# Hybrid attention block on one core: in the last unit the tensor engine keeps the program's order, with new places for transposes and products

## The chip, the cores and the metric

The kernel runs on one core of one Trainium2 chip. The metric is device time in microseconds of one execution, as the median of the runs shown. The core has four computing engines that matter here. TensorE does matrix products and transposes (PE in the profile, its weight loads PEld). VectorE (DVE) and ScalarE (ACT) move and compute elementwise. GpSimd (POOL) and SyncE (SP) mostly start DMAs. Each engine works off its own instructions in the order in which they stand in the program and waits at an instruction until what that instruction needs is there.

## The reference

The input is 512 tokens of width 1024, with 16 meta tokens put ahead. After a layer norm, one projection gives all that two attention branches and their gates need. The part that the change touches is the stick-breaking branch and what uses its result:

```python
def stick_breaking_block(q, k, v, q_pos):
    before = k_pos[None, :] < q_pos[:, None]
    z = jnp.einsum('bhqd,bhkd->bhqk', q, k) * (SB_HEAD_DIM ** -0.5)
    log_keep = jnp.where(before, jax.nn.log_sigmoid(-z), 0.0)
    suffix = lax.cumsum(log_keep, axis=3, reverse=True) - log_keep
    a = jnp.where(before, jnp.exp(jax.nn.log_sigmoid(z) + suffix), 0.0)
    return jnp.einsum('bhqk,bhkd->bhqd', a, v)
...
br_d = (y_d * silu(g_d)) @ w_br_diff
br_s = (y_s * silu(g_s)) @ w_br_sb
merged = sigmoid(m_d + b_gate[0]) * br_d + sigmoid(m_s + b_gate[1]) * br_s
h = layer_norm(DN_ALPHA * h + merged @ w_out, ln_g, ln_b)[:, N_META:]
```

## The kernel before

**Numbers and products.** Every float32 operand of a large product is split into a rounded part and a rest: a weight block `raw` gives `wh` (ScalarE, L183) and `wl` (VectorE, L188). A product is then three matmuls, high by high, high by rest and rest by high. One block is half of a projection, and `prep` splits it four blocks ahead of its use. A projection of 128 columns (`proj_tok`, L494 to L496) is 24 matmuls of 128x512 into one PSUM bank `ps`. Its pool `pj` has three banks.

**Units.** The attention is sixteen units: eight heads of the first branch (`d`), then eight pairs of heads of the stick-breaking branch (`s`). While a unit's attention runs, TensorE also computes projections for later units, and `run(proj, steps)` mixes the two. Each `yield` of a projection advances a clock of the program's own, and each step has a number on that clock at which it is written into the program. The numbers are in units of that clock and are no device times.

**One pair of heads.** For each of the two heads `c` of an `s` unit, `s_scores` makes logits in bank `sc` (L754), two sigmoids on ScalarE (L901, L903), a scan on VectorE (L907) and the attention weights `apad` (L908). `transposed` returns three parts: part 0 transposes four blocks into `t0` (L766), part 1 strips and three blocks into `t1` (L784, L766), part 2 three blocks into `t2`. After each part, ScalarE copies the bank to `ah` and VectorE subtracts to `al` (L771, L772), and part 2 also leaves a float32 block `af` (L802). The banks come from the pool `ptp`, which has two. `s_values` multiplies by the values into the single bank `av` (L916 to L924), ScalarE copies one half of it (`half`, L928), and VectorE adds (L930).

**The last unit.** It has no next unit to project for. Its five projections are `gd` 7, `md` 0, 1 and 2, and `gs` 7 (a gate projection, whose `silu` is L523, L524 and L526). Head `c`'s parts 0, 1, 2 stand at 7.0, 7.7 and 8.4 plus 6.5 times `c`, its product at 10.5 plus 6.5 times `c`.

**The late stage.** Behind the units, the attention's memory is given back (`early.close()` and the end of the pool `att`), and the pool `late` takes its place. First come seven projections, `md` 3 to 7 and `ms` 0 and 1, into `td` and `sm` by a sigmoid (L565). Mixed with them, `operands` builds from the finished first branch `ydT` four parts of `gh` and `gl` for the products of L1062: four elementwise steps on VectorE (L1037 to L1040), three casts to `gh` on ScalarE (L1043), and three subtractions to `gl` on VectorE (L1044).

**What sets the order.** Tile sorts the instructions of each engine by dependencies and expected times, so an instruction of the program may slip behind later ones. `follow` ties an instruction behind another of its engine. `keep_order(first, engines)` (L233) does so for all instructions from place `first` on: each keeps its place in the program's order on its engine. It is called for the start of the kernel and, for all engines, for the late stage. The units between are left to the sorting. The tie of the late stage binds its own instructions to each other, not to what is left of the last unit.

## Time and profile before

| | |
|---|---|
| median of 3 runs | 714.28 us (713.76 to 714.56) |
| the profiled execution | 716.97 us, of which 714.6 us are the span from first to last instruction |
| mean granted TensorE clock | 0.993 of full speed |
| TensorE busy | 698.9 us |
| VectorE busy | 571.8 us |
| ScalarE busy | 439.1 us |
| traffic | 123.36 MB by DMA |

In the views, start times count from the start of the span. A timeline row gives start, duration, engine, line, operation, output and inputs, and in brackets the idle time of the engine just before it and what ended it. A matmul's duration covers its way through the array, and the next one starts while it is still under way, so the pace of matmuls is read from start to start. In the views by window, PEclk is the granted share of TensorE's clock.

### The profile page before, as it was taken

Reading aid. Unit: us, or ns where it says so; the run is one execution under the profiler, and the core shown is the slowest. Engines: PE = TensorE matmul, PEld = TensorE weight load, DVE = VectorE, ACT = ScalarE, POOL = GpSimd, SP = SyncE. Lnnn points to the kernel's source line nnn. Section 1 sums busy time; section 2 is a strip of 40 time slices with the busy share of each in tenths; the row PEclk is TensorE's granted clock in tenths of the full one; section 3 lists DMA queues with packets and bytes.
Section 4 is the critical chain, followed back from the end, with each engine's and each line's share of the span. In section 5 each row is a group of like instructions: output and inputs, shape, how many; then the busy total and the mean of one; then the engine's idle time right before and its main releaser. Section 6 shows DMA issues by size and latency. Waiting matters only on the chain.

```text
span 714.6 us, 13390 instructions
## 1 busy us (share of the span) xinstructions
PE 698.9 (98%) x4494; PEld 637.0 (89%) x4494; DVE 571.8 (80%) x1265; ACT 439.1 (61%) x1065; POOL 125.9 (18%) x143
## 2 busy tenths in 40 slices
PE   8999999999999999999999999999989999999994
PEld 7999999989989898998989898888878998999884
DVE  6888898878788678988968989876296788788887
ACT  5776676757667687776848768666265446555300
POOL 3204210212222101212213110000012102130002
PEclk9999999999999999999999999999999999999998
DMA  9358854879987976999799875748249748696902
GB/s 292 95 166 164 177 129 121 185 180 192 191 204 167 225 178 154 192 208 217 197 205 197 203 171 139 199 113 253 79 130 181 150 126 185 136 191 174 321 15 103
DMA packets 182182, 123.36 MB, mean 173 GB/s; under 512 B 9009, under 2 KB 165074, under 8 KB 182114
## 3 DMA queue, kind: packets, MB, share of 16 engines
q1 hardware_dynamic: 148130, 102.32, 50.0%
q0 software_dynamic: 33664, 19.14, 21.4%
q10 hardware_dynamic: 320, 1.06, 0.4%
q8 instruction: 35, 0.57, 0.4%
q14 instruction: 33, 0.27, 0.1%
HBM read 91.96 MB, written 9.44 MB: 142 GB/s over the span
## 4 chain that ended last, share of the span: by engine, by line
PE 83%; DVE 8%; DMA 4%; ACT 3%; issue 1%; POOL 1%; SPq 0%; DVEq 0%; ACTq 0%; POOLq 0%
PE q L690 15%; PE ps L494 11%; PE ps L495 11%; PE ps L496 11%; PE q L1062 10%; PE ps L510 7%; PE sc L754 5%; PE t L766 3%; PE bank L385 1%; PE tv L723 1%; DMA raw<-in_w_in_dram 1%; DMA raw<-in_w_out_dram 1%; DMA lgb<-in_ln_g_dram 1%; DVE hr L1212 1%; DMA xt<-in_x_dram 1%
## 5 line engine op out<-in xcount | busy, mean ns | idle before, releaser
L494 PE MATMUL ps<-hTh,wh 128*128 128x512 f32 x368 | 145.5, 395 | 1.8 <-ACT wh L183 1.8
L188 DVE TENSOR_TENSOR wl<-raw,wh 128x512 fp32r<-128x512 f32 x169 | 115.5, 691 | 38.0 <-ACT wh L183 36.0
L495 PE MATMUL ps<-hTl,wh 128*128 128x512 f32 x368 | 145.3, 395 | 0.0
L496 PE MATMUL ps<-hTh,wl 128*128 128x512 f32 x368 | 145.2, 394 | 0.0
L183 ACT CAST wh<-raw 128x512 fp32r<-128x512 f32 x169 | 104.4, 625 | 30.2 <-PE ps L495 17.3
L494 PEld LDWEIGHTS ps<-hTh,wh 128*128 128x128 f32 x368 | 69.5, 189 | 15.4 <-ACT wh L183 2.2
L496 PEld LDWEIGHTS ps<-hTh,wl 128*128 128x128 f32 x368 | 69.6, 189 | 14.3 <-DVE wl L188 0.4
L495 PEld LDWEIGHTS ps<-hTl,wh 128*128 128x128 f32 x368 | 69.5, 189 | 13.4
L146 POOL DMA_DIRECT2D rawk<-in_w_in_dram x44 | 61.1, 1649 | 95.2 <-DMA rawk<-in_w_in_dram 50.5
L754 PE MATMUL sc<-k,A 128*128 128x264 f32 (+3 forms) x320 | 66.4, 300 | 0.0
L1062 PE MATMUL q<-gh,wh 128*128 128x256 f32 x224 | 63.5, 283 | 0.2 <-ACT t L1071 0.2
L1062 PE MATMUL q<-gl,wh 128*128 128x256 f32 x224 | 63.4, 283 | 0.0
L1062 PE MATMUL q<-gh,wl 128*128 128x256 f32 x224 | 63.4, 283 | 0.0
L907 DVE TENSOR_TENSOR_SCAN e<-e,diag 128x528 f32<-128x528 f32 (+1 forms) x64 | 53.5, 848 | 7.3 <-ACT e L901 7.2
L754 PEld LDWEIGHTS sc<-k,A 128*128 128x128 f32 x320 | 50.5, 189 | 3.2
L690 PE MATMUL q<-tS,wh 128*128 128x264 f32 x176 | 50.9, 290 | 0.9 <-DVE low L612 0.9
L690 PE MATMUL q<-tl,wh 128*128 128x264 f32 x176 | 50.2, 286 | 0.0
L690 PE MATMUL q<-tS,wl 128*128 128x264 f32 x176 | 50.2, 286 | 0.0
L772 DVE TENSOR_TENSOR al<-t,ah 128x512 fp32r<-128x512 f32 (+2 forms) x72 | 39.7, 552 | 12.5 <-ACT ah L771 8.6
L771 ACT CAST ah<-t 128x512 fp32r<-128x512 f32 (+2 forms) x72 | 34.2, 477 | 21.3 <-PE t L766 21.1
L510 PE MATMUL ps<-hTh,wh 128*128 128x264 f32 x160 | 46.4, 290 | 0.2 <-ACT k L632 0.2
L933 POOL DMA_DIRECT2D ys<-half x14 | 11.8, 840 | 196.2 <-ACT ys L932 109.7
(291 smaller groups left out, 1867.0 us busy)
## 6 DMA issues: line engine op xcount, KB each, us to landing
raw<-in_w_in_dram SPq DMA_DIRECT2D x141, 256.0 KB, 3.3
rawk<-in_w_in_dram POOLq DMA_DIRECT2D x44, 256.0 KB, 5.7
rawk<-in_w_in_dram SPq DMA_DIRECT2D x33, 256.0 KB, 3.8
k<-ks SPq DMA_DIRECT2D x60, 132.0 KB, 2.9
raw<-in_w_out_dram SPq DMA_DIRECT2D x16, 256.0 KB, 3.7
k<-ks SPq DMA_DIRECT2D x60, 66.0 KB, 2.6
A<-low SPq DMA_DIRECT2D x28, 128.0 KB, 3.0
raw<-in_w_br_diff_dram SPq DMA_DIRECT2D x12, 256.0 KB, 4.0
```

The lines of the kernel that those rows point to most:

```text
L146: second[l] = [lambda raw=raw, x=x: g.dma_start(raw, x, accum_op=ALU.add) for x in more]
L183: s.copy(wh, raw)
L188: eng.tensor_tensor(wl, raw, wh.bitcast(F32), op=ALU.subtract)
L494: pe.matmul(ps, wh[:, k % 4, :], hTh[:, k, M:], start=(k == 0), stop=False)
L495: pe.matmul(ps, wh[:, k % 4, :], hTl[:, k, M:], start=False, stop=False)
L496: pe.matmul(ps, wl[:, k % 4, :], hTh[:, k, M:], start=False, stop=(k == KT - 1))
L510: pe.matmul(ps[:, :H2], a[:, k % 4, :], b[:, k, ts(c, H2)], start=(k == 0 and m == 0), stop=(k == KT - 1 and m == 2))
L690: pe.matmul(bank, a[:, k, :], b, start=start and k == 0 and j == 0, stop=k == 3 and j == 2, skip_group_check=not start)
L754: pe.matmul(ps[:, :n], q, K[:, m, k0:k0 + n], start=(m == 0), stop=(m == 1))
L772: v.tensor_tensor(l, t[:, o:o + w], h.bitcast(F32), op=ALU.subtract)
L907: v.tensor_tensor_scan(rev, rev, diag[0][:, L - nk:][:, ::-1], 0.0, ALU.mult, ALU.max)
L1062: pe.matmul(bank, a[:, k, :], b[:, n, k, :], start=start and k == 0 and m == 0, stop=k == 3 and m == 2, skip_group_check=not start)
```

## The change

Two things are changed, both for the last unit alone. The steps of its two heads get numbers from a table `LAST` (parts 0, 1, 2 and the product, for each head): 13.0, 14.1, 18.2, 21.2 and 21.9, 21.9, 23.2, 24.9. And all instructions of TensorE (`ORDERED[:1]`) from the place in the program at 12.9 on keep the program's order, to the end of the kernel. The other engines are sorted in the last unit as they were.

```diff
+LAST = [13.0, 14.1, 18.2, 21.2], [21.9, 21.9, 23.2, 24.9]
...
                     parts = transposed(ta, apads[c])
-                    steps += [(7.0 + 6.5 * c + 0.7 * m, f) for m, f in enumerate(parts)]
-                    steps.append((10.5 + 6.5 * c, lambda c=c, ta=ta: s_values(unit, c, n, ta)))
+                    times = LAST[c] if last else [7.0 + 6.5 * c + 0.7 * m for m in range(3)] + [10.5 + 6.5 * c]
+                    steps += zip(times, parts)
+                    steps.append((times[3], lambda c=c, ta=ta: s_values(unit, c, n, ta)))
+                if last:
+                    steps.append((LAST[0][0] - 0.1, lambda: state.update(ends=len(nc.cur_bb.bb.instructions))))
             run(proj, steps)
...
+    keep_order(state["ends"], ORDERED[:1])
     keep_order(first, ORDERED + [mybir.EngineType.SP])
```

**The second head's product on TensorE.** In the kernel before, the product of head 1 (`av_6938`) is split: its first matmul L916 stands earlier, and the rest stands six matmuls into the third projection of the late stage (`ps_7121` is `md` 5, with `wh_7035` its first block):

```order
L494 MATMUL ps_7121<-hTh_149,wh_7035 128x512
L495 MATMUL ps_7121<-hTl_150,wh_7035 128x512
L496 MATMUL ps_7121<-hTh_149,wl_7036 128x512
L917 MATMUL av_6938<-af3_6919,v3_436 128x128
L918 MATMUL av_6938<-am_6898,v4_435 128x4x32
L922 MATMUL av_6938<-ah1_6900,V_6652 128x384
L923 MATMUL av_6938<-al1_6901,V_6652 128x384
L922 MATMUL av_6938<-ah2_6915,V_6652 128x256
L923 MATMUL av_6938<-al2_6916,V_6652 128x256
L924 MATMUL av_6938<-al0_6885,V_6652 128x512
```

In the changed kernel the same product (`av_6998`) stands in one piece, three matmuls ahead of the end of `gs` 7 (`ps_6916`), the last unit's last projection; six matmuls stand between the transposes of part 2 and it:

```order
L766 MATMUL t2_6982<-ident_129,apad1_434 128x128 x3
...
L496 MATMUL ps_6916<-hTh_149,wl_6818 128x512
L916 MATMUL av_6998<-ah0_6952,V_6652 128x512
L917 MATMUL av_6998<-af3_6990,v3_436 128x128
L918 MATMUL av_6998<-am_6963,v4_435 128x4x32
L922 MATMUL av_6998<-ah1_6965,V_6652 128x384
L923 MATMUL av_6998<-al1_6966,V_6652 128x384
L922 MATMUL av_6998<-ah2_6986,V_6652 128x256
L923 MATMUL av_6998<-al2_6987,V_6652 128x256
L924 MATMUL av_6998<-al0_6953,V_6652 128x512
```

Between the last place at which the two orders agree (the logits of 128x400 of head 1, L754) and the end of this product stand 120 projection matmuls before and 63 in the changed kernel. All else that stands there is the same work.

**ScalarE around it.** Before, the copy of head 1's product (`half_6947`) stands behind all else of the last unit and directly ahead of the late stage's first casts (`gh_7030`), which stand ahead of `md` 3's sigmoid (`td_7025`) and of the split of `md` 6's first block (`wh_7084`):

```order
L802 COPY af3_6919<-t2_6911 128x128
L928 COPY half_6947<-av_6938 64x512
L1043 CAST gh_7030<-ydT_6623 128x256
L1043 CAST gh_7030<-ydT_6623 128x2x256
L1043 CAST gh_7030<-t_7065 128x4x256
L565 ACTIVATE td_7025<-ps_7034,cols_144 128x512
L183 CAST wh_7084<-raw_6926 128x512
```

In the changed kernel the split of a block of `md` 5 (`wh_7053`) and the sigmoid of `gs` 7 (`sg_7013`) stand between the copy and the casts; from there on the order is as before. Ahead of the copy, the split `wh_7035` stands between the copies of part 1 and part 2:

```order
L771 CAST ah1_6965<-t1_6956 128x384
L183 CAST wh_7035<-raw_6801 128x512
L771 CAST ah2_6986<-t2_6982 128x256
L802 COPY af3_6990<-t2_6982 128x128
L928 COPY half_7007<-av_6998 64x512
L183 CAST wh_7053<-raw_6821 128x512
L523 ACTIVATE sg_7013<-ps_6916 128x512
L1046 CAST gh_7030<-ydT_6623 128x256
L1046 CAST gh_7030<-ydT_6623 128x2x256
L1046 CAST gh_7030<-t_7065 128x4x256
L565 ACTIVATE td_7025<-ps_7034,cols_144 128x512
L183 CAST wh_7084<-raw_6869 128x512
```

VectorE's rows follow the same pattern: the split `wl_7036` stands between part 1's `al` and part 2's `al`, and behind the sum L930 of head 1 stand `wl_7054`, the four elementwise steps and the two steps of the gate. GpSimd's and SyncE's rows stand in the same order in both kernels.

## Prediction

> **What bounds the kernel now.** I read the page first. It says which engine sets the time:

> ```profile
> span 714.6 us, 13390 instructions
> PE 698.9 (98%) x4494; PEld 637.0 (89%) x4494; DVE 571.8 (80%) x1265; ACT 439.1 (61%) x1065; POOL 125.9 (18%) x143
> ```

> TensorE is busy for 98% of the span, and the change takes no matmul away. So only stretches in which TensorE stands still, or runs below full clock, can be given back or added. The waits of TensorE alone, longest first, name the stretches:

> ```profile
> engine line waited for: us in total, times, longest us
> PE ps L494 <- ACT wh L183: 1.8, 1, 1.8
> PE warm L306 <- POOL ident masks.py:199: 1.4, 1, 1.4
> ```

> The longest wait of the whole kernel is one projection matmul that waits for a split weight block. The second row is the kernel's start. TensorE's timeline shows where the first one is:

> ```profile
> 516.83 0.39 PE L924 MATMUL av<-al,V 128*128 128x512 f32 x1
> 517.06 0.40 PE L494 MATMUL ps<-hTh,wh 128*128 128x512 f32 x1
> ...
> 520.96 0.39 PE L496 MATMUL ps<-hTh,wl 128*128 128x512 f32 x1
> 523.17 0.64 PE L494 MATMUL ps<-hTh,wh 128*128 128x512 f32 x1 [1.82 <-ACT wh L183]
> ...
> 526.66 0.46 PE L496 MATMUL ps<-hTh,wl 128*128 128x512 f32 x1
> 526.96 0.40 PE L494 MATMUL ps<-hTh,wh 128*128 128x512 f32 x1
> ```

> The first row is the end of the last unit's attention: the last matmul of head 1's product. Eighteen projection matmuls follow, then the wait, and behind it matmuls of 0.64 instead of 0.40 us. The windows around it say why:

> ```profile
> core 0: us, PE busy (x) PEld busy (x) DVE busy (x) ACT busy (x) POOL busy (x), PEclk, DMA share, GB/s
> 440.00:441.00 1.00, 0.64 (x5) 0.64 (x6) 1.00 (x3) 1.00 (x4) 0.00 (x0) 1.00 1.08 367
> 500.00:510.00 10.00, 10.00 (x51) 8.38 (x50) 3.59 (x7) 2.77 (x6) 0.00 (x0) 1.00 0.47 148
> 515.00:521.19 6.19, 6.19 (x31) 5.05 (x29) 3.16 (x7) 1.73 (x4) 0.00 (x0) 1.00 0.01 1
> 521.19:523.17 1.98, 0.16 (x1) 0.00 (x1) 1.80 (x3) 1.98 (x4) 0.00 (x0) 1.00 0.00 0
> 523.17:526.78 3.61, 3.61 (x9) 2.62 (x10) 3.26 (x8) 2.38 (x5) 0.00 (x0) 0.53 0.43 127
> ```

> The granted clock (PEclk) is 1.00 up to the wait and 0.53 for 3.6 us behind it. The wait costs twice: once standing still, once in a slow stretch. Why the block is late, ScalarE's and VectorE's timelines tell:

> ```profile
> 517.32 0.58 ACT L928 COPY half<-av 64x512 f32<-64x512 f32 x1 [5.75 <-PE av L924]
> 518.70 0.93 ACT L1043 CAST gh<-ydT 128x256 fp32r<-128x256 f32 x2 [0.81 <-DVE ysT L930]
> 520.98 1.04 ACT L1043 CAST gh<-t 128x1024 fp32r<-128x1024 f32 x1 [1.34 <-DVE t L1040]
> 521.93 0.68 ACT L565 ACTIVATE td<-ps,cols 128x512 f32<-128x512 f32 x1
> 522.51 1.12 ACT L183 CAST wh<-raw 128x512 fp32r<-128x512 f32 x2
> ...
> 517.93 0.69 DVE L930 TENSOR_TENSOR ysT<-av,half 64x512 f32<-64x512 f32 x1 [6.66 <-ACT half L928]
> 518.66 0.69 DVE L526 TENSOR_TENSOR ysT<-sg,ysT 128x512 f32<-128x512 f32 x1
> 519.27 0.42 DVE L1037 TENSOR_TENSOR t<-ydT 128x256 f32<-128x256 f32 x1
> ```

> ScalarE stands idle for 5.75 us until head 1's product is done, then copies it. The casts `gh` wait for VectorE's sum L930, which is the last reader of the memory that they go to, and only behind the casts and one sigmoid stand the splits `wh` for which TensorE waits. ScalarE had time for them, but they are queued behind a product that stands late on TensorE.

> **The change part by part.**

> *The wait.* First, what it costs. Without it, the matmul at 523.17 would have started one step after 520.96. A step is (520.96 - 517.06)/17 = 0.229 us. So 523.17 - 520.96 - 0.23 = 1.98 us are lost standing still. The nine slow matmuls take 526.96 - 523.17 = 3.79 us where nine steps take 2.06, and lose 1.73. Together 3.71 us.

> Then, whether it goes. From the last common place to the end of head 1's product, 63 projection matmuls stand instead of 120, and all else is equal. So the product ends 57 x 0.229 = 13.1 us earlier, with its last matmul's step at 517.06 - 13.1 = 504.0, if nothing new holds TensorE. The block `wh_7084` is the first of `md` 6, three projections or 72 matmuls behind `gs` 7. With three matmuls left of `gs` 7, it is needed at 504.0 + 75 x 0.229 = 521.2, as late as before, since the projections only trade places with attention work. When is it ready? The new rows ahead of it on ScalarE and VectorE take these durations, besides 0.69 for a split on VectorE (like L526):

> ```profile
> 501.92 0.59 ACT L523 ACTIVATE sg<-ps 128x512 f32<-128x512 f32 x1
> 502.65 0.69 DVE L524 TENSOR_TENSOR sg<-ps,sg 128x512 f32<-128x512 f32 x1
> ```

> The copy ends at 517.32 + 0.58 - 13.1 = 504.8. VectorE's queue from there is L930, the split `wl_7054`, two small steps, L524, one small step, L526 and one small step: 4 x 0.69 + 4 x 0.42 = 4.4 us, to 509.2. ScalarE's split and sigmoid lie within that. The last cast `gh` takes 1.04, to 510.3. Then the sigmoid `td` needs the end of `md` 3, at 504.0 + 27 x 0.229 = 510.2 and a matmul's way of 0.39: it ends about 511.3. The split ends half a microsecond later, at 511.9. That is 9 us ahead of 521.2. Before, it came 2 us too late. So the wait goes whole, with the slow stretch behind it: 3.7 us.

> What is late next? The other `gh` parts are queued on ScalarE behind sigmoids that follow TensorE's projections; each takes about 3 us with its waits, inside a projection's 24 x 0.229 = 5.5. The later blocks are split before the next part and stay ahead by about as much. Behind that, loads follow the freed buffers and so move with TensorE. I cost these at nothing; their cover is those 9 us.

> *The new order in the last unit.* TensorE now takes each transpose and each product at its written place, so all behind it on TensorE waits if it isn't ready. The tight places are the products' second matmuls L917, which need `af` of part 2, and head 1 is tighter: six matmuls lie between part 2 and its product, head 0 has fifteen. The same steps of head 1 in the trace of before:

> ```profile
> 509.85 0.49 PE L766 MATMUL t<-ident,apad 128*128 128x128 f32 x3
> 510.10 0.48 PE L916 MATMUL av<-ah,V 128*128 128x512 f32 x1
> 510.41 0.40 PE L494 MATMUL ps<-hTh,wh 128*128 128x512 f32 x1
> ...
> 510.44 0.37 ACT L771 CAST ah<-t 128x256 fp32r<-128x256 f32 x1 [3.79 <-PE t L766]
> 510.84 0.42 DVE L772 TENSOR_TENSOR al<-t,ah 128x256 fp32r<-128x256 f32 x1 [3.60 <-ACT ah L771]
> 511.30 0.27 ACT L802 COPY af<-t 128x128 f32<-128x128 f32 x1 [0.49 <-DVE al L772]
> ```

> From the start of part 2 to the end of `af` it took 511.57 - 509.85 = 1.72 us, on engines that stood idle before. TensorE reaches L917 after 0.25 for the transposes, 0.08 that the first matmul behind them takes more, six steps of 0.229 and one of 0.23 for L916: 1.93 us. The margin is 0.2 us. In the changed kernel a split stands on each engine ahead of part 2's copies, 0.69 us on VectorE. If it comes at its worst, `af` is 0.69 late and TensorE waits 0.5 us; if it comes in a gap, nothing. I take 0.2 us, since both engines are idle most of this time: 3.59 and 2.77 of 10 us busy in the window from 500 on. Such a wait costs its own length only:

> ```profile
> 440.37 0.39 PE L690 MATMUL q<-tS,wh 128*128 128x264 f32 x1 [0.63 <-DVE low L612]
> ```

> The window from 440 to 441, above, holds the end of this wait and shows the clock at 1.00. The other new waits have more room: head 0's product has nine matmuls or 2 us more than head 1's, and head 1's first transposes read weights that are finished long before. I cost them at nothing; if their cover is gone, each costs a few tenths.

> *Sum.* 3.7 less 0.2 is 3.5 us. The profiled execution took 716.97, of which 714.6 are span; it should come to 713.5. It lies 2.7 above the median of the runs, 714.28, and I take the same 3.5 off the median: 710.8 us.

> [...] The nine matmuls at 0.53 of the clock follow a gap of 2.2 us between two starts. [...]

> **The rivals.**

> *Short waits eat part of it.* Both heads' chains slip by half a microsecond to a microsecond each, as worked out above, without the clock falling. 0.8 to 2 us are lost: 711.4 to 712.6. For it speaks the margin of 0.2 us; against it, two engines that are idle for over half of that time.

> *The slow stretch stays.* If the clock falls for a reason of its own at about that time, only the 1.98 us come back, less 0.2: 712.5. [...] Against it speaks the row 523.17, which is slow from the first matmul behind the wait.

> *Nothing moves that TensorE waits for.* ScalarE's order from the casts on is as before, and if they wait for something other than head 1's product, the block is as late as before: 714.3. For it: the casts go to memory with many earlier readers. Against it: the idle times of 5.75 and 0.81 are ended by the product and by L930.

> *Slower: the fixed order makes waits as long as the one it removes.* The place is L917 of both heads. Today TensorE goes on with projections when `af` is late, because the sorting put the product further back; in the changed kernel it stands still. If `af` comes 1.8 us late at each head, the trace's price for such a wait is 3.7 us each: 7.4 - 3.7 = 3.7 us slower, 718.0. It decides once both waits together, with their slow stretches, pass 3.7 us. For that, head 1's chain would have to take 3.7 us instead of 1.72, so ScalarE or VectorE would have to be held for 2 us by something. Nothing in the window from 500 to 510 is that busy. [...]

> **How the numbers follow.** The forecast has a chance of 0.74, the short waits 0.12, the slow stretch that stays 0.04, nothing moved 0.06, slower 0.04. The prediction is 710.8 us. No new wait at all gives 710.6, and the runs of before spread by half a microsecond to each side at most, so the low end is 709.9. The high end, 712.6, takes in the short waits and the slow stretch that stays. The rest, 0.10, is left out. A measurement of this kernel can tell about 0.2% or 1.43 us from no change. The first three cases lie below 714.28 - 1.43 = 712.85: faster 0.90, same 0.06, slower 0.04.

> **What would show it.** The stage as it stands before:

> ```profile
> 520.00:530.00 10.00, 8.18 (x29) 6.02 (x29) 9.22 (x18) 7.50 (x13) 0.00 (x0) 0.83 0.43 126
> ```

> Right: in the changed kernel's trace, TensorE has no wait over 0.6 us behind the start stage, the granted clock stays at 1.00 between 500 and 560, head 1's copy `half` starts at about 504.2, ScalarE's first `gh` casts end near 510, and `md` 6 starts near 521 without a wait. The window from 520 to 530, with 29 matmuls before, then holds about 10/0.229 = 44. Wrong: a wait of TensorE at L917 or at a transpose L766 of the last unit of 1 us or more, a clock below 1.00 there, or the same wait for `wh` at a later projection.

## The result and the profile after

The changed kernel takes 712.15 us (median of 9 runs, 711.15 to 713.52), against 714.98 us of the kernel before on the same chip (9 runs, 713.76 to 716.88). The medians differ by 2.8 us and the means by 3.2. The measured ratio is 0.995, with a 95% interval from 0.9938 to 0.9962: 3.6 us less, with 2.7 to 4.4 us as the interval. It isn't the quotient of the two medians, which is 0.996, so a few tenths depend on how the runs are summed up. The changes given for the experiments below are taken from such ratios too. The profiled execution took 712.22 us. One execution of the kernel before in a later comparison took 765.0 us at a mean clock of 0.85; it is left out of all ratios and counts below.

The page of the changed kernel starts with:

```profile
span 710.4 us, 13389 instructions
PE 697.5 (98%) x4494; PEld 636.9 (90%) x4494; DVE 571.8 (80%) x1265; ACT 439.2 (62%) x1065; POOL 125.6 (18%) x143
```

The work is the same, and the span is 4.2 us shorter. The waits of TensorE in the changed kernel (engine, line, what it waited for, us in total, times, longest):

```profile
PE warm L306 <- POOL ident masks.py:199: 1.4, 1, 1.4
PE q L690 <- DVE low L612: 0.9, 2, 0.6
PE bank L339 <- DVE xn L335: 0.3, 1, 0.3
PE ps L510 <- ACT k L632: 0.2, 1, 0.2
PE q L1065 <- ACT t L1074: 0.2, 1, 0.2
```

The row of 1.8 us on `wh` is gone, and nothing has come in its place. L306 and L339 are the start stage, and L690 the wait at 440 that was there before. The windows of the changed kernel in the last unit and the late stage:

```profile
core 0: us, PE busy (x) PEld busy (x) DVE busy (x) ACT busy (x) POOL busy (x), PEclk, DMA share, GB/s
500.00:510.00 10.00, 10.00 (x50) 8.30 (x49) 7.28 (x16) 5.40 (x11) 0.00 (x0) 1.00 0.52 168
510.00:520.00 10.00, 10.00 (x45) 8.26 (x44) 5.49 (x10) 4.53 (x8) 0.00 (x0) 1.00 0.30 87
520.00:530.00 10.00, 10.00 (x46) 8.28 (x45) 8.21 (x14) 6.09 (x11) 2.67 (x2) 1.00 0.88 180
```

TensorE is busy without a gap at a granted clock of 1.00. The window from 520 on holds 46 matmuls where it held 29. VectorE has twice the work between 500 and 510 that it had there before (7.28 against 3.59 us), since the first part of `gh` and `gl` is now made there.

TensorE's timeline in the changed kernel at head 1's product and at the first block of `md` 6:

```profile
502.49 0.39 PE L916 MATMUL av<-ah,V 128*128 128x512 f32 x1
502.71 0.39 PE L917 MATMUL av<-af,v 128*128 128x128 f32 x2
...
503.64 0.39 PE L924 MATMUL av<-al,V 128*128 128x512 f32 x1
503.87 0.40 PE L494 MATMUL ps<-hTh,wh 128*128 128x512 f32 x1
...
520.91 0.39 PE L494 MATMUL ps<-hTh,wh 128*128 128x512 f32 x1
```

The product stands in one piece and waits for nothing at L917. The projection that waited before has no bracket, so nothing held it. ScalarE's timeline in the changed kernel has the same chain as before, 13 us earlier at the copy `half` and 12 us earlier at the last split:

```profile
501.35 0.37 ACT L771 CAST ah<-t 128x256 fp32r<-128x256 f32 x1
502.29 0.27 ACT L802 COPY af<-t 128x128 f32<-128x128 f32 x1 [0.57 <-DVE al L772]
504.12 0.58 ACT L928 COPY half<-av 64x512 f32<-64x512 f32 x1 [1.56 <-PE av L924]
504.72 0.62 ACT L183 CAST wh<-raw 128x512 fp32r<-128x512 f32 x1
505.25 0.59 ACT L523 ACTIVATE sg<-ps 128x512 f32<-128x512 f32 x1
505.74 0.92 ACT L1046 CAST gh<-ydT 128x256 fp32r<-128x256 f32 x2
508.84 1.06 ACT L1046 CAST gh<-t 128x1024 fp32r<-128x1024 f32 x1 [2.19 <-DVE t L1043]
510.23 0.69 ACT L565 ACTIVATE td<-ps,cols 128x512 f32<-128x512 f32 x1 [0.33 <-PE ps L496]
510.81 1.13 ACT L183 CAST wh<-raw 128x512 fp32r<-128x512 f32 x2
```

The copy `half` used to wait 5.75 us for the product; it now waits 1.56. The split that came 2 us too late ends at 511.9, nine microseconds ahead of its use at 520.91.

### The profile page after: what moved, and what is told of

It reads as the page before. It is cut to its first block, busy times and chain, and to the rows that moved or that the text cites. A ratio compares the mean times of both kernels' runs of the same rounds, so it can differ in the third digit from the quotient of the medians.

```text
span 710.4 us, 13389 instructions
## 1 busy us (share of the span) xinstructions
PE 697.5 (98%) x4494; PEld 636.9 (90%) x4494; DVE 571.8 (80%) x1265; ACT 439.2 (62%) x1065; POOL 125.6 (18%) x143
## 3 DMA queue, kind: packets, MB, share of 16 engines
q10 hardware_dynamic: 320, 1.06, 0.4%
## 4 chain that ended last, share of the span: by engine, by line
PE 86%; DVE 6%; DMA 3%; ACT 2%; issue 1%; POOL 1%; SPq 0%; ACTq 0%; DVEq 0%; POOLq 0%
PE q L690 16%; PE ps L496 12%; PE ps L494 12%; PE ps L495 12%; PE q L1065 10%; PE ps L510 7%; PE sc L754 6%; PE t L766 4%; DMA lgb<-in_ln_b_dram 1%; PE bank L385 1%; PE tv L723 1%; DVE hr L1215 1%; DMA xt<-in_x_dram 1%; PE av L922 1%; DMA raw<-in_w_out_dram 1%
## 5 line engine op out<-in xcount | busy, mean ns | idle before, releaser
L494 PE MATMUL ps<-hTh,wh 128*128 128x512 f32 x368 | 145.0, 394 | 0.0
L496 PE MATMUL ps<-hTh,wl 128*128 128x512 f32 x368 | 144.4, 392 | 0.0
L183 ACT CAST wh<-raw 128x512 fp32r<-128x512 f32 x169 | 104.4, 625 | 28.0 <-PE ps L495 15.3
L496 PEld LDWEIGHTS ps<-hTh,wl 128*128 128x128 f32 x368 | 69.2, 188 | 13.9
L495 PEld LDWEIGHTS ps<-hTl,wh 128*128 128x128 f32 x368 | 69.2, 188 | 13.1
L494 PEld LDWEIGHTS ps<-hTh,wh 128*128 128x128 f32 x368 | 69.2, 188 | 12.9
L754 PE MATMUL sc<-k,A 128*128 128x264 f32 (+3 forms) x320 | 65.9, 299 | 0.1
L1065 PE MATMUL q<-gh,wh 128*128 128x256 f32 x224 | 63.5, 283 | 0.2 <-ACT t L1074 0.2
L1065 PE MATMUL q<-gl,wh 128*128 128x256 f32 x224 | 63.4, 283 | 0.0
L1065 PE MATMUL q<-gh,wl 128*128 128x256 f32 x224 | 63.4, 283 | 0.0
L754 PEld LDWEIGHTS sc<-k,A 128*128 128x128 f32 x320 | 50.3, 189 | 3.3 <-ACT e L901 0.3
L690 PE MATMUL q<-tS,wh 128*128 128x264 f32 x176 | 50.9, 290 | 0.9 <-DVE low L612 0.9
L690 PE MATMUL q<-tl,wh 128*128 128x264 f32 x176 | 50.2, 286 | 0.0
L690 PE MATMUL q<-tS,wl 128*128 128x264 f32 x176 | 50.2, 286 | 0.0
L510 PE MATMUL ps<-hTh,wl 128*128 128x264 f32 x160 | 45.6, 286 | 0.0
L510 PE MATMUL ps<-hTl,wh 128*128 128x264 f32 x160 | 45.5, 285 | 0.0
```

The lines of the kernel that those rows point to most:

```text
L183: s.copy(wh, raw)
L494: pe.matmul(ps, wh[:, k % 4, :], hTh[:, k, M:], start=(k == 0), stop=False)
L495: pe.matmul(ps, wh[:, k % 4, :], hTl[:, k, M:], start=False, stop=False)
L496: pe.matmul(ps, wl[:, k % 4, :], hTh[:, k, M:], start=False, stop=(k == KT - 1))
L510: pe.matmul(ps[:, :H2], a[:, k % 4, :], b[:, k, ts(c, H2)], start=(k == 0 and m == 0), stop=(k == KT - 1 and m == 2))
L690: pe.matmul(bank, a[:, k, :], b, start=start and k == 0 and j == 0, stop=k == 3 and j == 2, skip_group_check=not start)
```

## The experiments

The prediction's theory is that the place of head 1's product on TensorE sets the wait: ScalarE takes its instructions in their order, and the split stands behind a copy that needs the product. In the expectations this theory has the letter A, and the other letters are its rivals, told where they are used. Each experiment was timed beside the kernel before, on the same chip.

### Head 1's product at four later places

The changed kernel keeps all of TensorE's rows in its new order, save the eight of head 1's product. They stand 54 (or 50, 45, 66) projection matmuls behind the end of `gs` 7. Only the number differs between the four kernels.

```diff
+            start = len(nc.cur_bb.bb.instructions)
...
+            if p == 7 and c == 1:
+                state["moved"] = {i.name for i in nc.cur_bb.bb.instructions[start:] if i.engine == ORDERED[0]}
...
-    keep_order(state["ends"], ORDERED[:1])
+    line = [i for i in nc.cur_bb.bb.instructions[state["ends"]:] if i.engine == ORDERED[0]]
+    late = [i for i in nc.cur_bb.bb.instructions[first:] if i.engine == ORDERED[0]]
+    moved = [i for i in line if i.name in state["moved"]]
+    line = [i for i in line if i.name not in state["moved"]]
+    at = line.index(late[54])
+    line[at:at] = moved
+    for one, other in zip(line[1:], line):
+        follow(one, other)
```

54, about where the product stood before:

> The changed kernel with one thing put back: head 1's product stands on TensorE where it stood before, 54 projection matmuls behind the end of gs 7; all other TensorE rows keep their new places. Theory A (the place of the product, with ScalarE's queue behind it, makes the wait): the wait for wh before md 6 is back with 1.98 us and the slow stretch with 1.7 us, so the time is that of the kernel before, within 0.5 us, and the gain is gone. Theory B (the kept order on TensorE is what helps, wherever this product stands): 3.6 us faster than before, no wait.

50, four matmuls earlier:

> As the run with the product 54 matmuls late, but 50 matmuls late. Theory A: the wait shrinks by 4 x 0.229 = 0.92 us to about 1.06 us. If the granted clock falls behind a wait of that length too, the kernel is 0.9 us faster than before; if it does not fall (theory A with a threshold between 1 and 2 us), 2.6 us faster. If the slow stretch has a cause of its own (theory C), it stands at the same time, around 523 us, with 1.7 us lost, whatever the wait. Theory B: no wait, 3.6 us faster.

45, nine matmuls earlier:

> As the run with the product 54 matmuls late, but 45 matmuls late. Theory A: the split is ready 0.1 us ahead of its use, so at most some tenths of waiting are left, for the second half of the split; clock at 1.00; within 0.5 us of the changed kernel, 3.2 to 3.7 us faster than before. Theory C: the slow stretch is still there, 2 us faster than before.

66, twelve matmuls later:

> As the run with the product 54 matmuls late, but 66 matmuls late. Theory A: the wait grows by 12 x 0.229 = 2.75 us to 4.7 us, with one slow stretch of about 1.7 us lost behind it (more if its length follows the wait): 2.7 us slower than before. Theory B: 3.6 us faster. Theory C: the slow stretch does not move with the wait.

The first block of `md` 6 on TensorE, with 54:

```profile
523.02 0.50 PE L494 MATMUL ps<-hTh,wh 128*128 128x512 f32 x1 [1.81 <-ACT wh L183]
```

With 50:

```profile
521.94 0.50 PE L494 MATMUL ps<-hTh,wh 128*128 128x512 f32 x1 [0.90 <-ACT wh L183]
```

With 66:

```profile
525.34 0.79 PE L494 MATMUL ps<-hTh,wh 128*128 128x512 f32 x1 [4.54 <-ACT wh L183]
```

With 45 no row of the waits names `wh`, and the longest wait behind the start stage is the old one at L690:

```profile
PE q L690 <- DVE low L612: 0.9, 2, 0.6
```

| place of the product | wait for `wh`, us | granted clock behind it | ratio to before (95%) | change, us |
|---|---|---|---|---|
| 45 | none | 1.00 (steps of 0.23 us) | 0.9959 (0.9945 to 0.9973) | -2.9 |
| 50 | 0.90 | 1.00 | 0.9978 (0.9964 to 0.9992) | -1.6 |
| 54 | 1.81 | 1.00 | 1.0003 (0.9993 to 1.0014) | +0.2 |
| 66 | 4.54 | 0.50 for 3.4 us | 1.0055 (1.0035 to 1.0075) | +3.9 |

Four matmuls are 4 x 0.229 = 0.92 us, and the wait falls by 0.91. Twelve are 2.75, and it grows by 2.73. So the place of the product alone sets the wait, microsecond for microsecond, and 54 alone brings the whole loss back. Theory A holds. What didn't come is the slow stretch: with 54 the wait is that of the kernel before, and the clock stayed at 1.00. This is taken up below.

### The late stage's parts at later places

To tell TensorE's order from ScalarE's queue: the kernel before, with the parts of `gh` and `gl` written 4.5 units later into the projections. TensorE's rows stand as before.

```diff
-        [(3.5 + 7.5 * i, f) for i, f in enumerate(parts)])
+        [(8.0 + 7.5 * i, f) for i, f in enumerate(parts)])
```

> The kernel before with one line changed: in the late stage the four parts of operands stand at 8.0 plus 7.5 each instead of 3.5 plus 7.5 each, so that on ScalarE the splits for md 6 stand ahead of the first gh casts. TensorE's order is row for row that of the kernel before, with head 1's product 54 matmuls late. Theory A (TensorE waits because the splits are queued behind that product on ScalarE): no wait before md 6, clock at 1.00, 3.7 us faster than before, as much as the change itself. Theory B: no gain, the time of the kernel before.

ScalarE's timeline in this kernel:

```profile
517.39 0.58 ACT L928 COPY half<-av 64x512 f32<-64x512 f32 x1 [5.75 <-PE av L924]
518.78 0.69 ACT L565 ACTIVATE td<-ps,cols 128x512 f32<-128x512 f32 x1 [0.81 <-DVE ysT L930]
519.37 1.13 ACT L183 CAST wh<-raw 128x512 fp32r<-128x512 f32 x2
520.39 0.93 ACT L1043 CAST gh<-ydT 128x256 fp32r<-128x256 f32 x2
```

The product is as late as before, and ScalarE waits the same 5.75 us for it. But the split now stands ahead of the casts and comes in time: no wait for `wh`, matmul steps of 0.23 us behind it as at a clock of 1.00, 712.66 us against 715.41, ratio 0.9962 (0.9947 to 0.9977), 2.7 us less. So no gain shows that TensorE's order brings by itself. What costs is the queue on ScalarE behind a late product.

If it is the same wait that both edits remove, their gains must not add up. The changed kernel with the same later parts:

> The changed kernel with the later operand parts as well (8.0 plus 7.5 each). Theory A: both edits take away the same wait, so together they give no more than either alone: within 0.5 us of the changed kernel, about 3 us faster than before. If they took away different losses, the gains would add to about 6 us.

712.72 us against 716.02, ratio 0.9957 (0.9944 to 0.997), 3.1 us less: within the intervals, one edit is worth as much as both.

### Each half of the change alone

The numbers of `LAST` alone, without the kept order:

```diff
-    keep_order(state["ends"], ORDERED[:1])
```

> The change's numbers alone, without keeping TensorE's order in the last unit: the sorting puts head 1's product 59 matmuls behind the end of gs 7, five more than before. Theory A: the wait grows by 5 x 0.229 = 1.15 us to 3.1 us, with the slow stretch behind it: 1.1 us slower than before. If the numbers by themselves helped, up to 3.6 us faster.

The sorting puts the product 59 matmuls behind the end of `gs` 7, five later than before. The first block of `md` 6 in this kernel:

```profile
524.43 0.50 PE L494 MATMUL ps<-hTh,wh 128*128 128x512 f32 x1 [2.95 <-ACT wh L183]
```

5 x 0.229 = 1.15 us more wait, on top of 1.82, is 2.97. It took 717.72 us, ratio 1.0035 (1.0022 to 1.0047), 2.5 us more than before, where 1.1 was expected. The new numbers alone are worse than the old.

The kept order alone, with the old numbers:

```diff
-LAST = [13.0, 14.1, 18.2, 21.2], [21.9, 21.9, 23.2, 24.9]
+LAST = [7.0, 7.7, 8.4, 10.5], [13.5, 14.2, 14.9, 17.0]
```

> The kept order alone, with the numbers of before (it is kept from the place at 6.9 on): the product of head 1 stands 39 matmuls ahead of the end of gs 7, so by theory A the wait before md 6 is gone, which gives 3.7 us. But head 0's first transposes now stand directly behind the values' transpose t4, whose bank they need; in the kernel before, that bank was read out 2.7 us after t4 started, so TensorE should wait about 2.6 us there, with a slow stretch of 1.7 us behind it, and for some tenths at both products: 0.6 to 2 us slower than before. Theory B: 3.6 us faster.

The late wait is gone, and TensorE stands at the first transposes of head 0 instead:

```profile
483.33 0.66 PE L766 MATMUL t<-ident,apad 128*128 128x128 f32 x4 [3.27 <-DVE v L744]
```

These need a bank that VectorE's L744 still reads. It took 719.33 us, ratio 1.0055 (1.0034 to 1.0076), 3.9 us more than before. That misses the expectation of 0.6 to 2 us more. The wait was 0.7 us longer than foreseen, and the late wait that went is worth 2.8 us and not the 3.7 counted for it, as worked out below. The 0.3 us at L917 and the half clock behind the wait (0.50 from 484.60 to 488.01) had been foreseen. Together that gives 3.27 + 0.30 + 2 x 0.16 + 1.73 - 2.8 = 2.8 us more, which lies in the interval of 2.4 to 5.4; the 1.1 us up to 3.9 stay open. The kept order puts the product early, and only the new numbers give each step the time that it needs.

### The slower rival's price

The prediction's slower rival needs steps that stand too close in the kept order. Here they follow each other with no projection between:

```diff
-LAST = [13.0, 14.1, 18.2, 21.2], [21.9, 21.9, 23.2, 24.9]
+LAST = [13.0, 13.0, 13.0, 13.0], [21.9, 21.9, 21.9, 21.9]
```

> The changed kernel with the three parts and the product of each head written at one place (13.0 and 21.9), with no projection matmul between them; the order is kept. The price of the slower rival: at each head t2 should wait about 1.1 us for t0's bank and L917 about 1.2 us for af, if the engines are free. That is 4.6 us for both heads, plus 1.7 us for each slow stretch if the clock falls: 4.6 to 8 us slower than the changed kernel, 1 to 4.5 us slower than before. The late wait before md 6 stays gone.

The waits of TensorE in this kernel:

```profile
PE t L766 <- DVE al L772: 4.0, 3, 2.7
PE av L917 <- ACT af L802: 3.9, 2, 2.9
```

It took 723.25 us, ratio 1.0108 (1.009 to 1.0126): 7.7 us more than before, and so some 11 more than the changed kernel. That misses the expectation of 1 to 4.5 us more than before. The waits stand where the rival had them, at L917 and at the transposes, but they come to about 8 us where 4.6 were expected. The clock stood at half for 6.83 us from the second wait on, in which TensorE was busy for 0.58 + 3.42 us; by an estimate from these rows (shown in the next section) half of that, 2 us, is lost, most of the rest. So the mechanism is real, and it is the distance between the steps in `LAST` that keeps it away.

### The slow stretch

With 54 the wait had come back without the slow stretch. Is that stretch a part of the wait? The kernel before was profiled three times more, unchanged. Two theories, D and E, stand against each other here. The 3.41 us of theory D are the length of the stretch in the first profile of this kernel, from 523.37 to 526.78, and its half is the wait there, 1.82 of 3.41 us; what the two have to do with each other is what the three profiles were to try.

> The kernel before, unchanged, looked at again. The wait of 1.8 us before md 6 had a slow stretch behind it in the first profile of this kernel and none in the run with the product 54 matmuls late. Theory D (the clock is judged in windows of 3.41 us that run free of the program, and falls when TensorE stands still for about half of one): the wait is there each time, with 1.8 us; the slow stretch of 3.41 us at half clock is there in some looks and missing in others, by where the windows' edges fall on the wait. Theory E (the kernel before always has it, and the other kernel's rows differ in something that prevents it): the slow stretch is there each time.

> As the first look: theory D some looks with and some without the slow stretch, the span shorter by about 1.7 us without; theory E always with.

> As the first look: theory D some looks with and some without the slow stretch, the span shorter by about 1.7 us without; theory E always with.

All three have the same wait (1.82, 1.82 and 1.81 us), but the clock fell only in the third. The changes of the clock lie whole multiples of one length apart. In the first profile of before, the clock falls at 523.366 and rises 3.413 us later. The first record of the clock, at 1.00, begins at 4.541, 518.83 us or 152 x 3.4133 ahead of the fall, and it falls again at 707.686, 184.32 us or 54 x 3.4133 behind it. In the profile of the changed kernel, 1.00 begins at 6.545 and ends at 702.864, and the 696.32 us between are 204 x 3.4133. I take these multiples as a raster. It stands elsewhere against the program in each execution: in the four profiles of before it has edges at 523.37, 522.63, 521.49 and 525.19, where the wait ends at 523.17, 523.49, 522.09 and 523.68. So I divided each trace at its raster and read how long TensorE stood still inside one raster window. First the window in which the wait ends or most of it lies, and then the next; the columns are those of the windows above, and the second number is TensorE's busy time. The kernel before, the profile of the prediction:

```profile
519.96:523.37 3.41, 1.59 (x8) 1.01 (x7) 3.17 (x7) 2.40 (x4) 0.00 (x0) 1.00 0.00 0
523.37:526.78 3.41, 3.41 (x9) 2.42 (x9) 3.06 (x7) 2.18 (x5) 0.00 (x0) 0.50 0.46 135
```

The first repetition:

```profile
519.22:522.63 3.41, 2.45 (x11) 1.69 (x9) 3.17 (x8) 2.07 (x4) 0.00 (x0) 1.00 0.01 2
522.63:526.04 3.41, 2.52 (x10) 1.77 (x11) 3.12 (x6) 3.25 (x7) 0.00 (x0) 1.00 0.15 40
```

The second:

```profile
518.08:521.49 3.41, 2.19 (x10) 1.50 (x8) 3.17 (x8) 2.07 (x4) 0.00 (x0) 1.00 0.01 2
521.49:524.90 3.41, 2.77 (x11) 1.99 (x12) 3.13 (x6) 2.99 (x7) 0.00 (x0) 1.00 0.23 67
```

The third:

```profile
521.78:525.19 3.41, 1.56 (x6) 0.94 (x6) 3.05 (x5) 3.41 (x7) 0.00 (x0) 1.00 0.00 0
525.19:528.60 3.41, 3.41 (x9) 2.63 (x9) 3.15 (x7) 1.89 (x5) 0.00 (x0) 0.50 0.79 223
```

Where the whole wait lies in one window (3.41 - 1.59 = 1.82 us idle, and 1.85 in the third repetition), the next window runs at half clock. Where an edge divides the wait in two (0.96 and 0.89 us, or 1.22 and 0.64), the clock stays at 1.00. With 54 it was divided into 0.94 and 0.91 us, and the clock stayed at 1.00 too. The kernel with steps too close gives the nearest case on the other side, and a second window in a row:

```profile
487.79:491.20 3.41, 0.78 (x4) 0.47 (x4) 3.41 (x8) 1.30 (x6) 0.00 (x0) 1.00 0.45 162
491.20:494.61 3.41, 0.58 (x3) 0.58 (x3) 2.48 (x7) 0.93 (x4) 0.00 (x0) 0.50 0.95 294
494.61:498.03 3.42, 3.42 (x12) 2.95 (x11) 0.68 (x1) 0.58 (x1) 0.00 (x0) 0.50 1.07 363
...
508.27:511.68 3.41, 1.82 (x12) 1.54 (x13) 1.59 (x4) 1.21 (x4) 0.00 (x0) 1.00 0.02 5
...
709.66:713.07 3.41, 1.77 (x15) 1.57 (x14) 2.90 (x6) 0.00 (x0) 0.66 (x1) 1.00 0.21 79
713.07:716.48 3.41, 0.00 (x0) 0.00 (x0) 3.26 (x8) 0.51 (x1) 1.23 (x3) 1.00 0.20 77
```

The row from 508.27 on has 3.41 - 1.82 = 1.59 us idle, and the clock did not fall behind it. The last two rows are the kernel's end, where TensorE runs out of work: with 3.41 - 1.77 = 1.64 us idle in the first of them the clock stayed at 1.00 in the second. The first profile of before and that of the changed kernel end at half clock, behind a window with 2.95 us idle in the one and 2.18 in the other. From the first record at 1.00 up to there, no other window of the two than that of the wait has more than 0.84 us idle, and the clock is at 1.00 throughout but for the stretch. So in the windows read here, up to 1.64 us of standing still left the clock at 1.00, and 1.82 us or more were followed by half of it. Between the two there is no case.

How often does the whole wait fall into one window? If the raster stands anywhere with the same chance, a wait of 1.82 us lies whole in one in (3.41 - 1.82)/3.41 = 47% of the executions. This is an estimate; if less than 1.82 us of one window were enough, it would be a little more. The runs agree: of 44 timed executions of the kernel before with their clocks listed, 20 have a mean granted clock of 0.993 or less, with a median span of 714.5 us, 22 have 0.995 or more, with 713.05 us, and two lie between. A window at half clock is worth 0.5 x 3.41/714 = 0.0024 of the mean. The mean also holds the half clock at the kernel's end, whose length varies (6.89 us in the first profile of before, 7.58 in that of the changed kernel), so the two groups are told apart only roughly: the four profiles of the kernel before have 0.993 and 0.994 with the stretch, 0.995 and 0.996 without. Of the changed kernel's nine runs none lies below 0.995; with the product at place 54, four of ten lie at 0.993 or less, and four at 0.995 or more.

## Why the prediction was right, point by point

**The number: inside the range, in part by luck.** Forecast were 710.8 us and a range up to 712.6; measured were 712.15. The upper part of that range stood for short waits and for a slow stretch that stays, and the changed kernel's trace shows neither. Of the difference of 1.35 us, half is a gain of 2.8 us between the medians where 3.5 were forecast (by the slow stretch, below), and half a kernel before that took 714.98 us in nine runs where the forecast started from 714.28 in three.

**The wait: right.** It was priced at 1.98 us and is gone. The four later places and the later parts show that it came from the product's place and from ScalarE's queue, both of which the prediction named.

**Its steps: right to a few tenths.** Predicted and found: the last step of the product ends at 504.0 and 503.87 (where the next matmul starts); the copy `half` starts at 504.2 and 504.12; last cast `gh` ends at 510.3 and 509.9; sigmoid `td` ends at 511.3 and 510.9; the split is ready at 511.9 and 511.9; needed at 521.2 and 520.91. The window from 520 has 46 matmuls for some 44 predicted.

**The new wait at L917: too dear, but near the edge.** I took 0.2 us, between 0 and 0.5, and it was 0. The split that could come ahead of part 2 did come, in VectorE's timeline of the changed kernel:

```profile
501.23 0.69 DVE L188 TENSOR_TENSOR wl<-raw,wh 128x512 fp32r<-128x512 f32 x1
501.84 0.42 DVE L772 TENSOR_TENSOR al<-t,ah 128x256 fp32r<-128x256 f32 x1
```

The cast `ah` before it ended at 501.72 (ScalarE's row of 501.35, above), so the split held `al` by 0.1 us at most. `af` ended at 502.56, and TensorE reached L917 at 502.71.

**The slow stretch: real, but in half of the executions only.** This is the term that was mis-sized. The prediction took 1.73 us of it as certain, from one profiled execution that had it. By the estimate above it costs about 0.47 x 1.73 = 0.8 us in the mean, which makes the whole gain 1.98 + 0.8 = 2.8 us. The four kernels without the wait gained 3.6 (the changed kernel), 3.1, 2.9 and 2.7 us; the interval of the changed kernel, 2.7 to 4.4, holds both 2.8 and the predicted 3.5. That the changed kernel's 3.6 lie 0.8 above 2.8 us isn't explained by any run, and needs no cause at this interval; its medians alone differ by 2.8. In the profiled pair, whose execution before had the stretch, the first product behind the late stage's projections (L1062 before, L1065 after) starts 4.05 us earlier on TensorE (542.67 against 546.72), of which 0.21 were there before the last unit's end (483.35 against 483.56 at the common logits): 3.84 us, for the 3.71 of the sum.

The expectations had counted the stretch as certain too, and so 45 (3.2 to 3.7 us faster expected), 50 (0.9 or 2.6 faster), 66 (2.7 slower), the later parts (3.7 faster) and the numbers alone (1.1 slower) came out by 0.3 to 1.4 us beside what was expected. The corrected price settles them. By the same estimate, a wait of 4.54 us puts 1.82 us or more into one window wherever the raster stands, and one of 2.95 us in about 80% of the cases; in the two profiles TensorE stood still for 3.41 and for 2.05 us of the window ahead of the half clock. So with 66 and with the numbers alone lost are 4.54 + 0.16 + 1.73 - 2.8 = 3.6 us (measured 3.9), and 2.95 + 0.16 + 1.73 - 2.8 = 2.0 (measured 2.5; nine of ten runs at 0.993 or less). With 50 the whole wait is 0.90 us, less than the 1.64 us behind which the clock stayed at 1.00, and it stayed there: 0.90 + 0.16 - 2.8 = -1.7 (measured -1.6). The 0.16 are what a wait costs beyond its bracket, 1.98 - 1.82.

**The rivals.** *The slow stretch has its own cause*: it fell. In the profiles that have the stretch ahead of the kernel's end, it starts at the edge behind a window in which TensorE stood still for 1.82 us (before), 1.85 (its third repetition), 2.05 (the numbers alone), 2.14 (the kept order alone), 2.63 (steps too close) and 3.41 us (66). In the changed kernel, without such a window, the clock is at 1.00 from 6.55 to 702.86; with 45 (from 522.13 on) and with the later parts, the matmul steps behind the place of the wait are 0.23 us. *Short waits*: none came. *Nothing moves*: it fell with the four places. *Slower by the fixed order*: its mechanism is real, +7.7 us when the steps follow each other directly, but the changed kernel leaves 0.15 us at its tightest place.

## What to carry to other kernels

When one engine waits for a small step of another, look at what stands ahead of that step in its queue: here a copy that waited for a late product held a split that had been ready to run, and moving either of the two removed the wait. The kept order on the bound engine paid here together with places that give each step its time; the order alone made this kernel 3.9 us slower and the places alone 2.5. Before pricing a stretch at half clock, take more than one profile: here the same wait of 1.81 or 1.82 us stood in all four profiles of the kernel before, and the stretch behind it in two of them.
